# Sample attention in steps of 512 keys with a maximum each, and three edits beside it, in a decoder step

## The chip, the cores and the metric

The kernel runs on one core of a Trainium2 chip. Its engines each work through their own instructions in order: TensorE (PE; its weight loads are listed apart, as PEld), VectorE (DVE), ScalarE (ACT), GpSimd (POOL) and SyncE (SP, which here only issues transfers). They wait for each other by semaphores. The metric is the device time of one execution in microseconds (us), lower is better; a time is quoted as the median of several runs.

## The reference

One step of a decoder layer, for 1024 prompt tokens of one sequence and for 8 sample sequences of 8 new tokens each, which have 2048 past tokens in paged caches:

```python
x = ffn_half(x, ...ffn1)                                   # x + 0.5 * (silu(h @ wg) * (h @ wu)) @ wd
q, kc, vc, ks, vs, kw, vw, gates, z, xbc, dtr = split_proj(rmsnorm(x) @ w_in)
o_att = g0 * o_cmp + g1 * o_sel + g2 * o_win               # 8 query heads, 2 KV heads, width 64
y_ssm = rmsnorm_per_group(ssd(...) * silu(z)) * ssm_norm   # Mamba-2 scan, 8 heads
x = x + concat(o_att, y_ssm) @ w_out
x = ffn_half(x, ...ffn2)                                   # and a final RMSNorm
```

Attention has three branches, each a softmax of its own. The compressed branch looks at summaries of blocks of 32 keys (127 of them for a sample sequence). Its probabilities rank the blocks of 64 keys, and the selected branch attends to the best 16 of them (`select_blocks`, `top_k`). The window branch attends to the last 512 keys. Sigmoid gates weigh the three. A softmax is `exp(s - max(s)) / sum`, so for several pieces of the keys, each with its own maximum, the numerators and sums have to be brought to one maximum before they are added. In the Mamba part `y * silu(z)` is normalised by the mean of its squares over each of two groups of 256 channels.

## The kernel before, in words

Feature rows lie on the 128 partitions, tokens on the free axis. The stages in time are: FFN1; from 753 us the projections by w_in, with the Mamba scan from 899 us and the gating from 1050 us among them; from 1176 us prompt attention with the compression of the sample caches in it (to 1583 us); sample attention with w_out in it (1583 to 1815 us); FFN2 and the last norm. Who runs when on an engine is set by a scheduler that reads the program with a modelled timeline, within what the pools' buffer counts allow; on the chip each engine then keeps that order. Matmuls of float32 are made of three (`mm3`, L237 to L239): each operand is split into a high part, made by a cast (`whi`, ACT), and a low part, the difference (`wlo`, a subtraction by `split`, L257). `sub`, `copy` and `scale` (L257, L254, L266) take the engine as a letter from the table `KN`: 'v' DVE, 'a' ACT, 'p' POOL.

**Sample attention** takes the 8 sequences as 4 pairs; a pair's 2 x 8 tokens x 8 heads are the 128 rows. For a pair:

- `choose` (L1821 to L1873) computes gates and compressed scores, and ranks the blocks by comparing all pairs of 31 block scores on 128x961 tiles: `cm` (greater, L1862), `ce` (equal, L1863), then `ce * tri` and `cm + ce` on POOL (L257), a row sum `rk` (L1867) and a mask `msk`, which PE transposes (`a_ps`, L1872). All four run ahead of the scores.
- `rows_in` (L1881) fetches keys and values in pieces of 512 keys for a sequence, into `schk`, 10 buffers: the window by a plain transfer on SP, the four pieces of the 2048 past keys by gathers that POOL issues (L1887). The gathers don't depend on `choose`; unselected blocks are masked in the scores.
- `scores` (L1894) works by branch. For each piece PE transposes the keys (`kT_ps`, copied to `skT` by ACT), multiplies (`s_ps`, two PSUM banks) and adds the mask (L1919); DVE adds the position bias and takes the maximum (L1922). After all four pieces (and the 8 new tokens per sequence, L1929) one maximum, one exp over 2112 columns on ACT (L1934), a sum, its reciprocal, the gate, and one scaling of S on DVE (L266).
- `values` (L1951) transposes S piece by piece (`sPT_ps`, one bank, shared with `a_ps`), copies (`sPT`) and adds the products into `so`; `compressed` (L1940) adds that branch and `outputs` (L1977) writes `qT`.

**w_out** (`out_w`, L2026; `out`) runs as PE's filling in the same stage: w_out comes in 32 pieces (the last 8 behind sample attention), loaded through SP into `raw`, a tile of two buffers which the squares of x (`x2_sq`, L2063) and rows of x on their way from and to DRAM (`xD`, L2092, L2095) use too. Low halves go to POOL and DVE in turn.

**Scan.** `BD`, one tile of 96x2x4x128, holds the decay terms as blocks, in three bf16 parts for two halves of the chunks (L1052 to L1058). The first matmul of the scan, `ar` (L1098), reads it.

**Gating** (`gate`, L1189): z is loaded (`za`, one buffer), multiplied onto y, and y's squares go into `ysq`, a buffer of the tag `nat`, which also holds rows on the way to the output; four `yn` matmuls (L1203) per chunk then sum them over the partitions.

Of the kernel before, what the change touches and what calls it, by code (L numbers as in the profile page):

```python
# [17 lines left out]
P = 128  # L18
# [15 lines left out]
PAST = 2048  # L34
B0AT = (0, 2, 4, 6)
EARLY = {(0, 0): (0, 128), (1, 0): (640,), (0, 1): (), (1, 1): (768,)}
KN = {'Bt': 'a', 'cb': 'a', 'de': 'vv', 'ea': 'pp', 'st': 'p', 'hT': 'v', 'xm': 'p', 'yz': 'v', 'ysq': 'a', 'kT': 'aa', 'sPT': 'v', 'S': 'vv', 'ce': 'p', 'cm': 'p', 'pcT': 'v', 'msk': 'a', 'osb': 'av', 'q': 'sspss', 'pb': ['apppaapp', 'apppappp', 'apppappp', 'apvpappp', 'apppapvp', 'appvappp', 'vpvvvpvv', 'pvvvvvvv'], 'pc': 'p', 'ob': 'aa', 'QA': 'aapv', 'QB': 'pv', 'chp': 'ap', 'th': 'aa', 'qt': (2, 7, 6, 5, 4, 3, 1, 0), 'cs': [3, 0, 2, 1, 1, 0, 1, 0]}
# [42 lines left out]
def hybrid_step(ctx: ExitStack, tc: tile.TileContext, *aps):  # L80
# [868 lines left out]
    def mamba_setup(K, K2, Q, acs_bank):  # L949
# [98 lines left out]
        BD = K.tile([96, 2, 4, P], BF16, name="BD", bufs=1)  # L1048
        r = Q.tile([96, 2, P], F32, name="bd_r", bufs=1)
        for u in range(3):  # L1050
            b = Q.tile([96, 2, P], BF16, name="bd_b", bufs=1)
            nc.vector.tensor_copy(b, r if u else q[:96])  # L1052
            d = slice(32 * u, 32 * u + 32)
            for z in range(2):
                nc.vector.tensor_tensor(BD[d, z], b[d, z:z + 1].to_broadcast([32, 4, P]),
                                        hm[d, :, None].to_broadcast([32, 4, P]), op=OP.mult)
            if u < 2:
                nc.vector.tensor_tensor(r, r if u else q[:96], b, op=OP.subtract)  # L1058
# [3 lines left out]
    def scan(K, dt, dA, U, Us, Bof, bm, mU, mUs, nacs, dend, cdec, dsk, sel, BD):  # L1062
# [5 lines left out]
        for c in range(9):  # L1068
# [25 lines left out]
            for g in range(2):  # L1094
                ar = b1("ar")
                arv = ar.rearrange("p (h l) -> p h l", h=4)
                if c < 8:
                    nc.tensor.matmul(ar, sel[:, 2 * (c % 4) + g:2 * (c % 4) + g + 1].to_broadcast([96, P]),  # L1098
                                     BD[:, c // 4].rearrange("p h l -> p (h l)"), start=True, stop=True,
# [89 lines left out]
    def gate(K, yr, c):  # L1189
# [5 lines left out]
        sq = K.tile([P, 4, P], F32, name="ysq", tag="nat")  # L1195
        if KN["ysq"] == "a":
            nc.scalar.activation(sq[:, :, :L], yT[:, :, ts], AF.Square)
        else:
            sub(KN["ysq"], sq[:, :, :L], yT[:, :, ts], yT[:, :, ts], OP.mult)
# [508 lines left out]

    def sample_attention():
        def b1(name):  # L1710
            return PSS.tile([P, 512], F32, name=name, tag="sPT_ps" if name == "a_ps" else name,
                            bufs=2 if name in ("kT_ps", "s_ps") else 1)
# [94 lines left out]
        for s4 in range(4):  # L1807
# [6 lines left out]
                                base=3, channel_multiplier=4)  # L1814
        grow = SC.tile([P, 4, 3], F32, name="grow")
# [59 lines left out]
        vals, probs = {}, {}  # L1875
# [5 lines left out]
        def rows_in(pr, br):  # L1881
            for s4 in range(4 if br == 0 else 1):
                for b in pair(pr):
                    chk = KS.tile([P, 4, 256], F32, name="schk")
                    vals[b, br, s4] = chk
                    if br == 0:
                        nc.gpsimd.indirect_dma_start(  # L1887
                            out=chk.rearrange("p s c -> p (s c)"), out_offset=None, in_=ch_sel,
                            in_offset=bass.IndirectOffsetOnAxis(ap=idx4[:, b, s4:s4 + 1], axis=0))
                    else:  # L1890
                        QUEUES[KN["q"][4]].dma_start(chk.rearrange("p s c -> p (s c)"),
                                          A["cache_win"][0, b].rearrange("(c s) k g d -> c (s k g d)", s=4))
# [418 lines left out]
```

## Time and profile before

| | |
|---|---|
| median of 3 runs | 2588.24 us (2579.92 to 2588.73) |
| the profiled execution | 2587.16 us |
| its span on the core | 2585.4 us |
| granted TensorE clock, mean | 0.966 |
| busy: PE / DVE / ACT / POOL | 2450.2 / 1751.9 / 1112.2 / 464.0 us |
| sample attention with w_out | 1583 to 1815 us |

The span is the time from the first to the last instruction on the core; the execution's time has a little around it. Busy times are sums of the instructions' durations, and "idle before" is what an engine stood before an instruction, with the event that ended it. The granted clock is a share of TensorE's full clock: at 0.5 a matmul takes twice as long.

### The profile page before, as it was taken

What the parts mean: (1) busy time and instruction counts of PE and PEld (TensorE: products, weight loads), DVE (VectorE), ACT (ScalarE), POOL (GpSimd) and SP (SyncE); (2) the same over time, 40 slices, a digit from 0 to 9 for tenths busy, and PEclk for the clock granted to TensorE, in tenths of its full rate; (3) what the DMA queues carried; (4) which work ended last, traced back from release to release, by engine and by line L of the source; (5) the groups of instructions that cost most, each with busy time, mean ns of one, the idle gap of its engine ahead of it and who ended that gap; (6) DMA issues with size and microseconds to landing.
All of it is one profiled execution on the core that took longest, in us unless ns stands there. A gap on an engine that the chain in (4) does not pass through costs nothing.

```text
span 2585.4 us, 48000 instructions
## 1 busy us (share of the span) xinstructions
PE 2450.2 (95%) x19011; PEld 2254.0 (87%) x19011; DVE 1751.9 (68%) x3610; ACT 1112.2 (43%) x2433; POOL 464.0 (18%) x549
## 2 busy tenths in 40 slices
PE   6999999999999999999999998788799999999998
PEld 5999999999999899897777775465699999999998
DVE  6776767677786645655666667644776767768776
ACT  7544444432152253225666664222444444443113
POOL 0000000011143334333443343322000000001110
PEclk9999999999999999899999997798799999999999
DMA  4334444596642224321101003176233434459754
GB/s 162 122 138 159 136 145 145 187 371 241 229 170 80 90 80 115 109 85 64 66 34 66 33 34 131 41 236 213 82 110 115 166 123 159 150 170 375 269 204 148
DMA packets 226269, 371.91 MB, mean 144 GB/s; under 512 B 18173, under 2 KB 143785, under 8 KB 224892
## 3 DMA queue, kind: packets, MB, share of 16 engines
q1 hardware_dynamic: 207112, 311.92, 35.5%
q0 software_dynamic: 7600, 38.59, 4.2%
q10 hardware_dynamic: 11332, 18.33, 1.9%
q8 instruction: 150, 2.46, 0.4%
q14 instruction: 75, 0.61, 0.1%
HBM read 250.84 MB, written 122.07 MB: 144 GB/s over the span
## 4 chain that ended last, share of the span: by engine, by line
PE 82%; DVE 8%; DMA 5%; ACT 3%; issue 1%; POOL 1%; SPq 0%; ACTq 0%; DVEq 0%; POOLq 0%
PE gY L352 6%; PE gY L353 6%; PE gY L351 6%; PE dq L609 6%; PE dq L608 6%; PE dq L610 6%; PE gX L352 5%; PE gX L351 5%; PE gX L353 5%; PE o L1688 3%; PE pT L1679 3%; DMA raw<-in_w_out_dram 1%; PE s L1641 1%; PE cA L1566 1%; PE xbc L237 1%
## 5 line engine op out<-in xcount | busy, mean ns | idle before, releaser
L609 PE MATMUL dq<-db,da 128*128 128x256 f32 (+1 forms) x1232 | 352.7, 287 | 0.3 <-DVE da L257 0.3
L610 PE MATMUL dq<-db,da 128*128 128x256 f32 (+1 forms) x1232 | 352.4, 287 | 0.0
L608 PE MATMUL dq<-db,da 128*128 128x256 f32 (+1 forms) x1232 | 349.1, 288 | 3.4 <-DMA db<-GD 1.7
L257 POOL TENSOR_TENSOR ds<-dw 128x512 f32<-128x512 f32 x22 | 29.0, 1319 | 1208.9 <-DMA dw<-in_ffn_wd_dram 512.8
L617 DVE TENSOR_TENSOR xT<-xT,dq 128x256 f32<-128x256 f32 (+1 forms) x456 | 186.8, 432 | 84.1 <-PE dq L610 82.4
L608 PEld LDWEIGHTS dq<-db,da 128*128 128x128 f32 x1232 | 229.8, 188 | 4.5 <-DVE Cc L371 1.4
L610 PEld LDWEIGHTS dq<-db,da 128*128 128x128 f32 x1232 | 232.2, 189 | 0.0
L609 PEld LDWEIGHTS dq<-db,da 128*128 128x128 f32 x1232 | 231.2, 188 | 0.6 <-DVE da L257 0.5
L254 ACT CAST whi<-ws 128x512 fp32r<-128x512 f32 x156 | 96.4, 622 | 209.2 <-PE gY L353 144.1
L257 DVE TENSOR_TENSOR wlo<-raw,whi 128x512 fp32r<-128x512 f32 x168 | 115.8, 694 | 85.1 <-ACT whi L254 84.8
L254 ACT CAST da<-ds 128x512 fp32r<-128x512 f32 x88 | 52.6, 624 | 236.6 <-PE dq L610 93.5
L254 ACT CAST whi<-raw 128x512 fp32r<-128x512 f32 x184 | 113.7, 624 | 75.2 <-DMA raw<-in_w_out_dram 37.6
L1657 ACT ACTIVATE pb<-s,mx 128x256 f32<-128x256 f32 (+3 forms) x192 | 105.2, 553 | 73.1 <-DVE mx L1655 38.2
L257 DVE TENSOR_TENSOR wlo<-ws,whi 128x512 fp32r<-128x512 f32 x156 | 106.7, 687 | 42.8 <-ACT whi L254 42.3
L1679 PEld LDWEIGHTS pT<-ident,pb 128*128 128x128 f32 x528 | 59.8, 143 | 43.4 <-issue 39.5
L1654 DVE TENSOR_REDUCE mx<-s 128x1 f32<-128x384 f32 (+2 forms) x128 | 66.7, 536 | 43.2 <-PE s L1646 32.2
L351 PE MATMUL gX<-B6h,whi 128*128 128x256 f32 (+1 forms) x320 | 92.2, 289 | 1.3 <-ACT Cc L358 1.3
L264 POOL TENSOR_TENSOR pb<-pb,sm 128x640 f32<-128x640 f32 (+7 forms) x70 | 84.9, 1236 | 45.8 <-DVE sm L1664 43.6
L352 PE MATMUL gX<-B6h,wlo 128*128 128x256 f32 (+1 forms) x320 | 92.5, 289 | 0.5 <-DVE wlo L257 0.5
L351 PE MATMUL gY<-B3h,whi 128*128 128x256 f32 (+1 forms) x320 | 91.5, 287 | 1.4 <-ACT whi L254 1.4
L352 PE MATMUL gX<-B7h,wlo 128*128 128x256 f32 (+1 forms) x320 | 91.8, 287 | 0.3 <-DVE wlo L257 0.3
L353 PE MATMUL gX<-B6l,whi 128*128 128x256 f32 (+1 forms) x320 | 92.0, 288 | 0.0
(705 smaller groups left out, 8648.8 us busy)
## 6 DMA issues: line engine op xcount, KB each, us to landing
db<-GD SPq DMA_DIRECT2D x42, 1632.0 KB
GD<-Cc SPq DMA_DIRECT2D x154, 272.0 KB
GD<-his SPq DMA_DIRECT2D x84, 272.0 KB
raw<-in_ffn_wg_dram SPq DMA_DIRECT2D x22, 1024.0 KB
raw<-in_ffn_wu_dram SPq DMA_DIRECT2D x22, 1024.0 KB
dw<-in_ffn_wd_dram SPq DMA_DIRECT2D x44, 512.0 KB
GD<-hp SPq DMA_DIRECT2D x70, 272.0 KB
db<-GD SPq DMA_DIRECT2D x14, 1088.0 KB
```

The source lines that it names most:

```text
L254: return nc.scalar.copy(out, src) if eng == "a" else ENGINES[eng].tensor_copy(out, src)
L257: ENGINES[eng].tensor_tensor(out, x, y, op=op)
L264: nc.gpsimd.tensor_tensor(out, x, by.to_broadcast(list(x.shape)), op=OP.mult)
L351: nc.tensor.matmul(q, ah[:, k], b_, start=first, stop=False, skip_group_check=True)
L352: nc.tensor.matmul(q, al[:, k], b_, start=False, stop=False, skip_group_check=True)
L353: nc.tensor.matmul(q, ah[:, k], c_, start=False, stop=(k == 3), skip_group_check=True)
L608: nc.tensor.matmul(q, x, bh[:, u, o], start=first, stop=False, skip_group_check=True)
L609: nc.tensor.matmul(q, y, bh[:, u, o], start=False, stop=False, skip_group_check=True)
L610: nc.tensor.matmul(q, x, bl[:, u, o], start=False, stop=(u == np_ - 1), skip_group_check=True)
L617: nc.vector.tensor_tensor(x, x, q, op=OP.subtract if i == 4 else OP.add)
L1657: nc.scalar.activation(pb[:, st:st + pn], s, AF.Exp, bias=mx[:, 0:1], accum_out=part[:, hh_, i:i + 1])
L1679: nc.tensor.transpose(tq_[:kn, P * hh_:P * hh_ + P], src, ident)
```

## The change

**Steps.** Sample attention becomes 20 steps: for each pair the window (k = 0) and then the four pieces of 512 past keys (k = 1 to 4); the new tokens go with k = 0 and k = 4, which are 576 wide. Each step has its own maximum (`nm[:, k]`), exp and sum (`rs[:, k]`), and S isn't scaled. Its values go to 64 columns of their own in the bank `so`, which one bf16 matmul with a zero operand clears for a pair; 320 to 383 hold the compressed branch. At a pair's end `outputs` takes the least of the negated maxima of k = 1 to 4, makes factors by an exp, sums, divides, applies the gates and adds the five pieces with `scalar_tensor_tensor`. Values of a step are written behind the scores of the next. Rows are fetched five steps ahead. `choose` for a pair stands behind k = 1 of the pair before it.

**Banks.** `s_ps` has one bank instead of two, and `a_ps` one of its own; `kT_ps` keeps two, `sPT_ps` and `so` one each.

**GpSimd.** `ce` and `cm` go to DVE. So do w_out's low halves, except for the last 8 pieces, where POOL takes every second one. **w_out's buffers**: `raw` has three buffers for w_out alone, and `xs` two for the squares and x's rows.

**Gating.** Squares are written over `za` by ACT, DVE adds them in pairs, and there are two `yn` matmuls instead of four. **Scan.** `BD` becomes two tiles, made one after the other.

```diff
-KN = {... 'ysq': 'a', 'S': 'vv', 'ce': 'p', 'cm': 'p', ...}
+AHEAD = 5
+KN = {... 'ce': 'v', 'cm': 'v', ...}
...
+        BD = []
+        def blocks_of(z):
+            D = K.tile([96, 4, P], BF16, name=f"BD{z}", bufs=1)
+            r = Q.tile([96, P], F32, name="bd_r", bufs=1)
+            for u in range(3):
+                b = Q.tile([96, P], BF16, name="bd_b", bufs=1)
+                src = r if u else q[:96, z]
+                nc.vector.tensor_copy(b, src)
+                if u < 2:
+                    nc.vector.tensor_tensor(r, src, b, op=OP.subtract)
+                d = slice(32 * u, 32 * u + 32)
+                nc.vector.tensor_tensor(D[d], b[d, None, :].to_broadcast([32, 4, P]),
                                         hm[d, :, None].to_broadcast([32, 4, P]), op=OP.mult)
+            BD.append(D)
...
-        sq = K.tile([P, 4, P], F32, name="ysq", tag="nat")
-            nc.scalar.activation(sq[:, :, :L], yT[:, :, ts], AF.Square)
+        nc.scalar.activation(za[:, :, :L], yT[:, :, ts], AF.Square)
+        nc.vector.tensor_tensor(za[:, ::2, :L], za[:, ::2, :L], za[:, 1::2, :L], op=OP.add)
         q = side("yn")
         for g in range(2):
-            for i in range(2):
-                nc.tensor.matmul(q[:L, g:g + 1], sq[:, 2 * g + i, :L], ones[:, :1], start=(i == 0), stop=(i == 1),
-                                 skip_group_check=True)
+            nc.tensor.matmul(q[:L, g:g + 1], za[:, 2 * g, :L], ones[:, :1], start=True, stop=True,
+                             skip_group_check=True)
...
+        def scores(pr, k, nm, rs):
+            n = 512 + (TS if k in (0, 4) else 0)
+            S = K.tile([P, 576], F32, name="S", bufs=4)
+            mx = K.tile([P, 2], F32, name="smxs", bufs=4)
...
+            nc.vector.tensor_reduce(nm[:, k:k + 1], mx[:, :2 if n > 512 else 1], axis=AX.X, op=OP.max, negate=True)
+            nc.scalar.activation(S[:, :n], S[:, :n], AF.Exp, bias=nm[:, k:k + 1], accum_out=rs[:, k:k + 1])
+            return S, n
...
+        def outputs(pr, O, nm, rs):
+            nc.vector.tensor_reduce(t[:, 0:1], nm[:, 1:5], axis=AX.X, op=OP.min)
+            nc.scalar.activation(cf[:, 1:5], nm[:, 1:5], AF.Exp, scale=-1.0, bias=t[:, 0:1])
...
             osb = K.tile([P, 64], F32, name="osb")
-            copy("a", osb, O[:, :64])
+            copy("a", osb, O[:, 320:384])
+            for k in range(5):
+                nc.vector.scalar_tensor_tensor(osb, O[:, 64 * k:64 * k + 64], cf[:, k:k + 1], osb, op0=OP.mult,
+                                               op1=OP.add)
...
+        for i, (pr, k) in enumerate(steps):
+            if i + AHEAD < len(steps):
+                rows_in(*steps[i + AHEAD])
+            now = scores(pr, k, *state[pr][:2])
+            if held is not None:
+                finish()
+            held = pr, k, *now
+            if k == 1 and pr < 3:
+                choose(pr + 1)
+        finish()
...
-        raw = WA.tile([P, 576], F32, name="raw", bufs=2)[:, :512].rearrange("p (k f) -> p k f", k=4)
+        raw = WA.tile([P, 4, P], F32, name="raw", bufs=3)
...
-        split(hi, lo, raw, "pv"[m % 2 == 0])
+        split(hi, lo, raw, eng)
...
-    ws = [out_w(WA, 0, m) for m in range(KD)]
+    ws = [out_w(WA, 0, m, "vp"[m % 2]) for m in range(KD)]
```

How the order moves, at three places. POOL in sample attention: before, gathers, low halves and the choices' two passes stand in one queue (the first eight gathers are those of the first pair).

```order
L1887 DMA schk<-in_cache_sel_dram,idx_18705 128x1024 x8
L257 TENSOR_TENSOR wlo<-raw,whi 128x512
L257 TENSOR_TENSOR ce<-ce,tri 128x961
L257 TENSOR_TENSOR cm<-cm,ce 128x961
L257 TENSOR_TENSOR wlo<-raw,whi 128x512 x2
L257 TENSOR_TENSOR ce<-ce,tri 128x961
L257 TENSOR_TENSOR cm<-cm,ce 128x961
L257 TENSOR_TENSOR wlo<-raw,whi 128x512 x3
```

After, the same stretch of POOL's queue is all its 32 gathers, and then the four low halves of the last pieces:

```order
L1895 DMA schk<-in_cache_sel_dram,idx_18702 128x1024 x32
L258 TENSOR_TENSOR wlo<-raw,whi 128x512 x4
```

The passes on `ce` and `cm` now stand on DVE, between a step's drain of scores (L1927, written ISA), copies of transposed S (L255), additions onto x (L2071) and a low half; this is the second pair's choice:

```order
L1870 TENSOR_TENSOR cm<-imp 128x961
L1871 TENSOR_TENSOR ce<-imp 128x961
L1856 MEMSET pg 128x1
L258 TENSOR_TENSOR ce<-ce,tri 128x961
L1927 ISA S,smxs<-s_ps,bsel 128x512
L1927 ISA smxs 128x1
L2071 TENSOR_TENSOR xT_20106<-xT_20106,wout 128x512
L258 TENSOR_TENSOR cm<-cm,ce 128x961
L258 TENSOR_TENSOR wlo<-raw,whi 128x512
L255 COPY sPT<-sPT_ps 128x512
```

PE at the stage's end, from the last w_out matmul of the stage to the norm's first (`nps`), after the change: values of four pieces (`so`, 16 matmuls each) follow each other, and scores of the last two steps stand before them.

```order
L240 MATMUL wout<-ol,whi 128x288
L1973 MATMUL so<-schk,sPT 32x64 x16
L1959 MATMUL sPT_ps<-ident,S 64x128
L1918 MATMUL s_ps<-skT,QS 64x512 x2
L1924 LDWEIGHTS mskT
L1924 MATMUL s_ps<-oneh,mskT 128x512
L1970 MATMUL so<-vtok,sPT 32x64 x4
L1963 MATMUL sPT_ps<-ident,S 128x128 x4
L1932 MATMUL s_ps<-ksTs,QS 64x64 x2
L1973 MATMUL so<-schk,sPT 32x64 x16
L1963 MATMUL sPT_ps<-ident,S 128x128 x4
```

Before, the transposes of keys, three more score matmuls and five pieces' values stood there (they are in the rows of time that the next section shows).

More of the change, by code (lines that the diff above doesn't have):

```diff
@@ L1706, in hybrid_step @@
     PSS = Es.enter_context(pool("sa_ps", bufs=1, space=PSUM))
+    PSA = Ahead(PSS)
+    for nm_ in ("a_ps", "s_ps", "sPT_ps", "so", "kT_ps"):
+        PSA.first(nm_, [P, 512], 2 if nm_ == "kT_ps" else 1)
     def sample_attention():
         def b1(name):
-            return PSS.tile([P, 512], F32, name=name, tag="sPT_ps" if name == "a_ps" else name,
-                            bufs=2 if name in ("kT_ps", "s_ps") else 1)
+            return PSA.tile(name, [P, 512], 2 if name == "kT_ps" else 1)
         ch_sel = A["cache_sel"][0].rearrange("n (c s) k g d -> (n c) (s k g d)", s=4)
@@ L1873, in choose @@
             copy(KN["msk"], mskT[:, pr], q[:32, :P])
-        vals, probs = {}, {}
+        vals = {}
         def group_rows(pr):
             return [(slice(64 * (b % 2) + 32 * g, 64 * (b % 2) + 32 * g + 32), b, g) for b in pair(pr) for g in range(2)]
-        def rows_in(pr, br):
-            for s4 in range(4 if br == 0 else 1):
-                for b in pair(pr):
[L1884 to L1892, printed above, removed]
@@ new lines, in rows_in @@
+        def rows_in(pr, k):
+            for b in pair(pr):
+                chk = KS.tile([P, 4, 256], F32, name="schk")
+                vals[b, k] = chk
+                if k:
+                    nc.gpsimd.indirect_dma_start(
+                        out=chk.rearrange("p s c -> p (s c)"), out_offset=None, in_=ch_sel,
+                        in_offset=bass.IndirectOffsetOnAxis(ap=idx4[:, b, k - 1:k], axis=0))
+                else:
+                    QUEUES[KN["q"][4]].dma_start(chk.rearrange("p s c -> p (s c)"),
+                                      A["cache_win"][0, b].rearrange("(c s) k g d -> c (s k g d)", s=4))
@@ L1948, in compressed, with values @@
                                  skip_group_check=True)
             return O
-        def values(pr, br, O, last):
-            nt = 4 if br == 0 else 1
-            S = probs.pop(br)
-            for s4 in range(nt + 1):
-                new = s4 == nt
+        def values(pr, k, S, n, O):
+            for new in range(2 if n > 512 else 1):
                 q = b1("sPT_ps")
@@ L2061, in x2_sq @@
         else:
-            sq = WA.tile([P, 576], F32, name="raw", bufs=2)[:, :c]
+            sq = WA.tile([P, 576], F32, name="xs", bufs=2)[:, :c]
             nc.scalar.activation(two(sq), x, AF.Square)
             nc.vector.tensor_tensor(acc2[z], acc2[z], sq, op=OP.add)
-    for _ in sample_attention():
-        pass
+    sample_attention()
     PO = Es.enter_context(pool("psum_wo", bufs=2, space=PSUM))
@@ L2089, in hybrid_step @@
         w = out_w(WA, 1, m)
[L2090 removed]
+        xs = WA.tile([P, 576], F32, name="xs", bufs=2)
         for b in range(2):
```

154 lines of the change are left out of this document (66 added, 88 removed).

## The prediction

> **What bounds the kernel now.** I read first the page (span, share of TensorE, chain), then the table by stretches, then the waits, and last the order of time at the places that these name.
>
> ```profile
> span 2585.4 us, 48000 instructions
> PE 2450.2 (95%) x19011; PEld 2254.0 (87%) x19011; DVE 1751.9 (68%) x3610; ACT 1112.2 (43%) x2433; POOL 464.0 (18%) x549
> PEclk9999999999999999899999997798799999999999
> ```
>
> TensorE (PE) is busy for 95% of the span and its clock is near full but in a few slices: 7 at slices 25 and 26, 8 and 7 at slices 28 and 29. A slice is 64.6 us, so these five begin at 1551 us and hold sample attention, where I looked by stretches. The columns are start and end, length, then busy us of PE, PEld, DVE, ACT and POOL, the granted clock, the DMA share and GB/s.
>
> ```profile
> 1583.00:1601.00 18.00, 12.65 (x56) 6.32 (x55) 9.31 (x29) 8.31 (x21) 8.90 (x9) 0.81 0.97 348
> 1601.00:1643.00 42.00, 39.07 (x182) 26.44 (x183) 33.55 (x75) 15.72 (x31) 15.79 (x8) 1.00 0.32 95
> 1643.00:1684.00 41.00, 24.35 (x75) 16.86 (x74) 21.13 (x40) 5.99 (x13) 11.45 (x6) 0.64 0.07 20
> 1684.00:1787.00 103.00, 90.16 (x1012) 65.17 (x1012) 44.54 (x114) 32.35 (x56) 30.00 (x29) 0.96 0.73 234
> 1787.00:1815.00 28.00, 18.47 (x249) 10.71 (x248) 11.23 (x31) 5.99 (x11) 1.27 (x1) 0.70 0.54 174
> ```
>
> Two stretches are poor: 1643 to 1684, where PE is busy for 24.35 of 41 us at a clock of 0.64 while DMA is all but idle (0.07), and 1787 to 1815, 18.47 of 28 at 0.70. In 1684 to 1787 PE still stands for 12.8 us. What ended the idle time, by waits (total us, times, longest):
>
> ```profile
> POOL wlo L257 <- ACT whi L254: 62.8, 9, 12.2
> POOL schk L1887 <- PE so L1974: 45.9, 6, 13.7
> PE wout L237 <- ACT whi L254: 12.1, 7, 4.0
> ACT raw L2063 <- DVE msk L1870: 21.0, 2, 10.5
> PE a_ps L1872 <- DVE msk L1870: 9.6, 3, 4.9
> PE sPT_ps L1963 <- DVE S L266: 4.4, 1, 4.4
> ```
>
> GpSimd (POOL) does gathers and the low halves of w_out in one queue: a low half waits for its high half (62.8 us), a gather for a buffer (45.9), and each holds up what is queued behind it. PE itself waits for the block choice's mask (9.6), for w_out's high half (12.1) and once for the scaling of S (4.4).
>
> **The first poor stretch.** The last three block choices run there one after another. One of them, from the chain of work, and PE beside it:
>
> ```profile
> 1648.51 1.16 DVE cm L1862
> 1650.88 2.25 POOL ce L257
> 1655.45 1.15 DVE rk L1867
> 1657.34 0.40 PE L1872 MATMUL a_ps<-ident,msk 128*32 128x128 f32 x1 [4.94 <-DVE msk L1870]
> 1661.60 0.63 PE L239 MATMUL wout<-ol,whi 128*128 128x512 f32 x1
> 1662.03 0.63 PE L237 MATMUL wout<-oh,whi 128*128 128x512 f32 x1
> 1642.74 0.39 PE L237 MATMUL wout<-oh,whi 128*128 128x512 f32 x1
> 1642.97 0.39 PE L238 MATMUL wout<-oh,wlo 128*128 128x512 f32 x1
> ```
>
> PE stands 4.94 us for the mask, and its matmuls then come 0.43 us apart instead of 0.23. Counted at full clock the stretch has 24.35 x 0.64 = 15.6 us of PE work, in 41 us.
>
> After the change, the choice for a pair stands among the steps of the pair before it, so this work can lie between transposes and scores. The pace I take for the whole of 1643 to 1787 (144 us) comes from the rows beside it: 15.6 + 90.16 x 0.96 = 102.2 us of work at full clock. The stretch from 1684 on needs 103 us for 86.6, 1.19 per us of work; 1601 to 1643 needs 42 for 39.07, 1.075. At 1.075 the 144 us become 110 (-34), at 1.19 they become 122 (-22). What raises the pace is VectorE (DVE):
>
> ```profile
> L257 POOL TENSOR_TENSOR wlo<-raw,whi 128x512 fp32r<-128x512 f32 x13 | 18.3, 1405 | 63.0 <-ACT whi L254 62.8
> L257 DVE TENSOR_TENSOR wlo<-raw,whi 128x512 fp32r<-128x512 f32 x14 | 10.7, 764 | 8.7 <-ACT whi L254 8.7
> L266 DVE TENSOR_SCALAR S<-S,mxs 128x2112 f32<-128x2112 f32 x4 | 6.9, 1720 | 0.1
> L266 DVE TENSOR_SCALAR S<-S,mxs 128x576 f32<-128x576 f32 x4 | 2.1, 526 | 0.1
> L1934 ACT ACTIVATE S<-S,mxs 128x2112 f32<-128x2112 f32 x4 | 8.2, 2058 | 6.2 <-DVE mxs L1933 6.2
> L1929 DVE CUSTOM_DVE_ANT_0 S<-s_ps,bnew 128x64 f32<-128x64 f32 x8 | 1.8, 219 | 0.0
> L1922 DVE CUSTOM_DVE_ANT_0 S<-s_ps,bsel 128x512 f32<-128x512 f32 x16 | 11.0, 688 | 8.9 <-PE s_ps L1919 8.7
> DMA to landing us min/median/max: 4.4/5.8/9.1
> ```
>
> Added to DVE: 12 low halves at 0.764 (9.2 us) and 8 operations on ce and cm; the trace has no such pass with two wide inputs on DVE, so between the 1.16 of L1862 (same output) and POOL's 2.25, and I take 1.16, the same engine (9.3). The recombination is 20 passes of 128x64 out of PSUM at 0.219 and some 28 tiny ones, which I bound by nothing and the same 0.219 and take at 0.16 (8.9). Removed: 4 x 1.72 + 4 x 0.526 (-9.0); small maxima and reciprocals go both ways and are costed at nothing. DVE goes from 119.8 us (its five stretches) to about 138, in some 200 us: it still has room, but in an in-order queue with more in it. Against that, PE's 12.1 us for high halves shrinks with a third w_out buffer. I take 1.205, nearer the measured 1.19: 123, and 1 us for the four matmuls that zero the sums (bounds 0 and 4 x 0.4, the mask transpose). **Term 1: -20** (bounds -34 and, at 1.33, -7). The new maxima and the extra exps, 20 instead of 8, go on DVE and ACT beside PE; the exp is cut from 2.06 us per 2112 keys to a fraction per 512, off PE's path while PE has other columns to do. Gathers now stand alone in POOL's queue and are issued five steps ahead, before a transfer is needed; at 0.07 to 0.73 DMA share there is room, so I cost this at nothing. Without that cover it would be one landing, 5.8 us, per pair. The first two stretches hold the loads (0.97) and a PE that is already full: 0.
>
> **The second poor stretch.** From the last w_out matmul to the norm's first matmul:
>
> ```profile
> 1786.76 0.29 PE L239 MATMUL wout<-ol,whi 128*128 128x288 f32 x1
> 1800.70 1.11 PE L1963 MATMUL sPT_ps<-ident,S 128*128 128x128 f32 x4 [4.37 <-DVE S L266]
> 1802.60 1.08 PE L1974 MATMUL so<-schk,sPT 128*32 128x64 f32 x32 [0.78 <-DVE sPT L254]
> 1803.62 1.12 PE L1963 MATMUL sPT_ps<-ident,S 128*128 128x128 f32 x4
> 1815.10 1.20 PE L807 MATMUL nps<-ones,acc 128*128 128x1 f32 x5 [0.76 <-DVE qT L1987]
> ```
>
> 28.3 us: one exp over four chunks and a scaling stand between the last scores and the first values, then five value chunks at 2.92 us each (1800.70 to 1803.62, at half clock). Now only the last two steps' scores and four value chunks follow the last w_out matmul: 4 x 2.92 = 11.7, two steps' scores at 1 each (estimates, from a chunk's share of the rows here), the value matmuls of the pair's first chunk and the new rows, 2 more, and the recombination, 5 x 0.22, a transpose and the 0.76 that the norm waits for qT, some 2.5: about 18 to 19. **Term 2: -9** (bounds -3, if the exp waits stay, and -12 at full clock).
>
> **Blocks for the scan and the gating.** The two tiles of the decay blocks:
>
> ```profile
> 894.28 1.28 DVE L1055 TENSOR_TENSOR BD<-bd_b,hm 32x512 bf16<-32x512 bf16 x2
> 899.16 1.01 PE L1098 MATMUL ar<-BD,sel 96*128 96x512 bf16 x2 [6.39 <-DVE BD L1055]
> ```
>
> PE waits 6.39 us for six block passes of 0.64 and what lies between. The first matmuls now need only three passes: 3 x 0.64 = 1.9 less, and half of the casts' work, 0.6. **Term 3: -2.5** (bounds 0 and -5, when PE's half clock behind it goes too). In the gating, squares need no free output buffer any more:
>
> ```profile
> 1055.93 1.15 ACT L1197 ACTIVATE ysq<-yT 128x512 f32<-128x512 f32 x2 [6.30 <-DMA out_dram<-nat]
> 1054.00:1058.00 4.00, 2.25 (x17) 2.02 (x16) 1.77 (x7) 1.72 (x4) 0.52 (x1) 0.92 0.16 41
> 1058.00:1068.00 10.00, 10.00 (x49) 10.00 (x48) 2.81 (x6) 2.43 (x4) 2.54 (x2) 0.50 0.45 121
> ```
>
> The squares waited 6.30 us for an output transfer, PE stood 1.75 of 4 us, and then ran ten us at 0.50, which costs 5 us of full-clock work. All of it back is -7; but z's one buffer is now held until the sums are made, and the next z load with what is queued behind it on SP comes later, up to +4. DVE's pair sum (0.7 to 1.3 us by the wide passes above) adds itself to that chain. **Term 4: -5** (bounds -10, with the next slow stretch, and +4). [...]
>
> Sum: -20 - 9 - 2.5 - 5 = **-36.5**. The profiled execution took 2587.16 us (1.8 around its span), 1.1 below the median of 2588.24. So 2587.2 - 36.5 = 2550.7, on the median's basis **2552 us**.
>
> **The rivals.** *DVE's queue becomes the pace.* A step's score drain (0.69) and the copy of its transposes stand in order behind the choice's five passes of 1.16 and w_out's low halves. For: the DVE sum grows by 18 us and ce and cm come in the middle of steps. Against: 138 us of about 200, and other PE work between. At a pace of 1.33 (term 1 is -7) with the other terms the sum is -23, 2565; with the gating's +4 2574. *PE never stands long enough to lose its clock.* For: the half clock follows each poor place shown. Then pace 1.075: -33, tail -11, scan and gating -11: 2533. *The choice and its GpSimd passes were not what held the stage* but w_out's loads, whose waits are the same whoever splits them: term 1 is -2, the tail -5, half of terms 3 and 4 -4, in all -11: 2577, no change that can be told. *The other side: one bank for scores.* Before, two banks let the next scores start while DVE drains; now there is one. It is used 20 + 8 times, and the bank for the transposes of S as often. If each holds PE for one drain and its hand-over, the 0.78 us of the row at 1802.60, that is 56 x 0.78 = 44 us, 2596; if the clock in the stage also falls to the 0.81 of the first stretch, 102.2 x (1/0.81 - 1/0.96) = 20 more, 2615. It decides from 36.5 / 56 = 0.65 us per use. Against it: no row shows PE waiting for that drain, the transposes' bank was single before, and values of the step before and w_out columns stand between two uses. [...]
>
> **How the numbers follow.** Forecast 0.47, DVE's queue 0.20, full clock 0.13, loads 0.12, one bank 0.08. The range goes from 2530 (the pace of 1.075 with the bounds of the small terms) to 2580 (loads). The likeliest case alone: 2541 to 2563. 0.5% is 13 us, about what a measurement of this kernel can tell from no change: faster means under 2575. The forecast, the first two rivals and a quarter of loads are faster, 0.83; the rest of loads, and little of the last, the same, 0.10; slower 0.07.
>
> **What would show it.** Right: the norm's first matmul comes near 1779 instead of 1815; no stretch in the stage under a clock of 0.8 but the tail; the waits of PE on the mask and of POOL's wlo gone; the tail's 28.3 near 19; PE's wait on the first blocks about 4 us; and no squares waiting on an output transfer. Wrong: PE waiting on a score drain or on a DVE copy for tens of us, gathers waiting to land, or a stretch of z loads before the yn matmul. If the stage keeps its 230 us with less POOL time, the third rival holds.

## The result

The changed kernel takes **2546.19 us** (median of 4 runs, 2545.51 to 2548.51), the kernel before 2586.31 us beside it (4 runs): a ratio of **0.985, 95% interval 0.983 to 0.987**, 40 us less. Forecast were 2552 us, with 2530 to 2580 as the range. The sum came out; its parts did not, as the table below shows. All medians and ratios are of runs in the chip's usual state, which leaves out one run of the experiments, 8164.42 us of the kernel "changed, old banks".

The page of the changed kernel, the lines that answer to those of before:

```profile
span 2546.8 us, 48004 instructions
PE 2439.3 (96%) x18979; PEld 2241.6 (88%) x18979; DVE 1759.6 (69%) x3676; ACT 1116.8 (44%) x2461; POOL 430.4 (17%) x530
PEclk9999999999999999999999999899899999999999
```

TensorE is busy 11 us less with nearly as many instructions. More of them ran at full clock: no slice is at 7 now, two are at 8. Sample attention by stretches (start and end, length, busy us of PE, PEld, DVE, ACT, POOL, granted clock, DMA share, GB/s):

```profile
1584.00:1604.00 20.00, 15.50 (x50) 8.03 (x50) 12.05 (x44) 6.41 (x22) 9.32 (x10) 0.50 0.51 179
1604.00:1644.00 40.00, 38.58 (x287) 24.89 (x285) 31.61 (x78) 17.96 (x39) 1.90 (x2) 0.90 0.66 214
1644.00:1684.00 40.00, 40.00 (x322) 27.08 (x311) 27.16 (x74) 19.23 (x40) 6.92 (x6) 1.00 0.52 159
1684.00:1724.00 40.00, 36.16 (x350) 26.74 (x349) 27.43 (x69) 15.30 (x31) 10.53 (x8) 0.91 0.72 232
1724.00:1765.00 41.00, 39.76 (x409) 30.43 (x398) 25.65 (x76) 14.32 (x32) 9.37 (x9) 1.00 0.75 239
1765.00:1780.00 15.00, 9.09 (x207) 5.52 (x206) 8.86 (x31) 2.86 (x8) 0.00 (x0) 0.97 0.57 180
```

The hole is gone: from 1604 to 1765 us PE stands for 6.5 of 161 us, at 0.9 to full clock. The poor row is now the first: the end of prompt attention runs at half clock, and sample attention begins later than before.

To see where time went, I cut every profile at four instructions: w_in's first matmul, prompt attention's first score matmul (`s`) and last value matmul (`o`), and the norm's first (`nps`). For the kernel before and then the changed one, the stretch of prompt attention and that of sample attention:

```profile
1176.40:1590.10 413.70, 397.31 (x2642) 286.37 (x2641) 273.87 (x683) 266.76 (x716) 163.36 (x246) 0.97 0.11 42
...
1590.10:1815.10 225.00, 179.16 (x1542) 123.30 (x1541) 116.08 (x275) 65.63 (x122) 61.83 (x48) 0.86 0.52 169
```

```profile
1174.00:1603.80 429.80, 408.66 (x2641) 291.18 (x2641) 275.05 (x683) 267.36 (x716) 164.56 (x249) 0.95 0.12 44
...
1603.80:1780.00 176.20, 163.79 (x1547) 114.65 (x1545) 120.72 (x327) 69.66 (x150) 28.71 (x25) 0.96 0.66 209
```

Sample attention lost 48.8 us: 33.4 in which PE stood, and 15.4 of busy time for the same number of matmuls (1542 and 1547), the clock being 0.96 instead of 0.86. Prompt attention, in which no line was changed, grew by **16.1 us**. With the other stretches (all from one profile each, in us):

| kernel | w_in to `s` | prompt | sample | after `nps` | span |
|---|---|---|---|---|---|
| before | 422.9 | 413.7 | 225.0 | 770.3 | 2585.4 |
| changed | 418.2 | 429.8 | 176.2 | 766.8 | 2546.8 |
| difference | -4.7 | +16.1 | -48.8 | -3.5 | -38.6 |

The rest of the difference, +2.3, is in front of w_in, where the two programs do the same.

### The profile page after: what moved, and what is told of

Same layout as the page of the kernel before. It is cut to its first block, busy times and chain, and to the rows that moved or that the text cites. A ratio compares the mean times of both kernels' runs of the same rounds, so it can differ in the third digit from the quotient of the medians.

```text
span 2546.8 us, 48004 instructions
## 1 busy us (share of the span) xinstructions
PE 2439.3 (96%) x18979; PEld 2241.6 (88%) x18979; DVE 1759.6 (69%) x3676; ACT 1116.8 (44%) x2461; POOL 430.4 (17%) x530
## 4 chain that ended last, share of the span: by engine, by line
PE 83%; DVE 8%; ACT 3%; DMA 3%; issue 1%; POOL 0%; ACTq 0%; DVEq 0%; SPq 0%; POOLq 0%
PE gY L353 6%; PE gY L354 6%; PE gY L352 6%; PE dq L609 5%; PE dq L610 5%; PE dq L611 5%; PE gX L353 4%; PE gX L354 4%; PE gX L352 4%; PE o L1691 3%; PE pT L1682 3%; PE s L1644 1%; PE cA L1569 1%; PE xbc L238 1%; PE cA L1571 1%
## 5 line engine op out<-in xcount | busy, mean ns | idle before, releaser
L255 ACT CAST whi<-ws 128x512 fp32r<-128x512 f32 x156 | 96.4, 622 | 210.5 <-PE gY L354 144.7
L258 DVE TENSOR_TENSOR wlo<-raw,whi 128x512 fp32r<-128x512 f32 x180 | 123.0, 688 | 79.2 <-ACT whi L255 78.9
L255 ACT CAST da<-ds 128x512 fp32r<-128x512 f32 x88 | 52.8, 626 | 236.9 <-PE dq L611 92.5
L255 ACT CAST whi<-raw 128x512 fp32r<-128x512 f32 x184 | 113.9, 625 | 65.9 <-PE gY L354 20.0
L1682 PE MATMUL pT<-ident,pb 128*128 128x128 f32 x528 | 90.8, 290 | 3.5 <-ACT pt L255 1.5
L353 PE MATMUL gY<-B3h,wlo 128*128 128x256 f32 (+1 forms) x320 | 91.7, 287 | 0.2 <-DVE wlo L258 0.2
L353 PE MATMUL gY<-B2h,wlo 128*128 128x256 f32 (+1 forms) x320 | 91.8, 287 | 0.0
```

The lines of the kernel that those rows point to most:

```text
L255: return nc.scalar.copy(out, src) if eng == "a" else ENGINES[eng].tensor_copy(out, src)
L258: ENGINES[eng].tensor_tensor(out, x, y, op=op)
L353: nc.tensor.matmul(q, al[:, k], b_, start=False, stop=False, skip_group_check=True)
L1682: nc.tensor.transpose(tq_[:kn, P * hh_:P * hh_ + P], src, ident)
```

## The experiments

Three questions were open: what makes prompt attention longer; what carries the gain in sample attention (the steps, the place of the choices, GpSimd's freed queue, the buffers or the banks); and what the parts give together. Each run's profile was cut as above; "sample + after" adds the last two stretches, because a kernel can move w_out columns behind `nps`.

| kernel | median, us | ratio to before [95%] | w_in to `s` | prompt | sample + after |
|---|---|---|---|---|---|
| before | 2586 to 2592 | 1 | 422.9 | 413.7 | 995.3 |
| changed, again | 2544.8 | 0.984 [0.981, 0.987] | 418.5 | 428.5 | 940.5 |
| changed, old gating | 2538.9 | 0.980 [0.979, 0.982] | 427.3 | 413.7 | 940.7 |
| before, new gating and blocks | 2603.5 | 1.005 [1.003, 1.007] | 416.8 | 430.5 | 997.5 |
| changed, work back on GpSimd | 2547.2 | 0.983 [0.981, 0.985] | 419.3 | 429.8 | 945.0 |
| changed, old buffers | 2557.1 | 0.987 [0.985, 0.989] | 419.5 | 428.0 | 950.5 |
| changed, choices ahead | 2540.3 | 0.984 [0.982, 0.987] | 414.9 | 430.1 | 935.6 |
| before with the steps alone | 2551.3 | 0.988 [0.985, 0.990] | 419.4 | 412.6 | 961.8 |
| changed, old banks | 2579.4 | 0.997 [0.995, 0.999] | 417.4 | 428.3 | 968.7 |
| before, new banks | 2566.2 | 0.991 [0.988, 0.994] | 417.9 | 415.4 | 975.2 |
| before, new banks, buffers, GpSimd | 2561.2 | 0.989 [0.986, 0.992] | 417.8 | 412.6 | 968.7 |
| changed, old gating, choices ahead | 2533.1 | 0.979 [0.976, 0.982] | 427.3 | 410.8 | 939.2 |
| changed, rows two steps ahead | 2542.4 | 0.982 [0.979, 0.985] | 416.7 | 430.7 | 942.0 |

The kernel before was timed beside each group of four; its median was 2588.3, 2586.7 and 2591.8 us.

### The gating and prompt attention

The changed kernel with the gating's lines as before:

```diff
-        nc.scalar.activation(za[:, :, :L], yT[:, :, ts], AF.Square)
-        nc.vector.tensor_tensor(za[:, ::2, :L], za[:, ::2, :L], za[:, 1::2, :L], op=OP.add)
+        sq = K.tile([P, 4, P], F32, name="ysq", tag="nat")
...
+            nc.scalar.activation(sq[:, :, :L], yT[:, :, ts], AF.Square)
...
```

> The changed kernel with the gating as before (squares into a buffer of the tag nat, four matmuls per chunk); PE's order in prompt attention is then that of the kernel before. Theory 1: the gating edit cost more than it gave, because with it the scheduler laid out prompt attention anew, and from its first score matmul to its last value matmul it took 16 us longer (429.8 against 413.7). Then this kernel is faster than the changed one by about 11 to 14 us: 2532 to 2536, with that stretch near 414. Rival: the longer stretch comes from sample attention's own setup and banks reaching into it, and the gating's gain of 2 to 5 us is lost here: 2548 to 2551, with the stretch near 430.

Measured: 2538.9 us, ratio 0.980, and prompt attention back at 413.7 us. Theory 1 holds for that stretch. The time fell by less than the 16 us, because the stretch from w_in to `s` grew to 427.3 us: with the old gating and the two block tiles together the scheduler lays out that stretch in a third way.

The kernel before with the gating's and the blocks' edits (both as in the diff of the change) and nothing else:

> The kernel before with the gating edit and the two block tiles, and nothing else; PE's order in prompt attention is then that of the changed kernel. Theory 1 (the gating edit's new layout of prompt attention costs about 16 us, the two edits' own gain is 4 to 5): 2586 + 11 = about 2597, slower than before. Rival (the prediction's terms 3 and 4, and no cost in prompt attention): 2579.

Measured: 2603.5 us (9 runs), ratio 1.005 [1.003, 1.007]: **slower than before** by half a percent, as theory 1 had it (2597), and clear of the rival. Its prompt attention:

```profile
1173.80:1604.30 430.50, 408.35 (x2641) 290.60 (x2641) 275.14 (x683) 268.00 (x716) 164.96 (x248) 0.95 0.12 45
```

The same 430 us and the same clock of 0.95 as in the changed kernel, without any of sample attention's edits. PE's order in prompt attention is word for word the same in all kernels with the new gating and blocks, and the same in all with the old gating as in the kernel before; between the two it differs throughout. So the gating edit reaches prompt attention through the order that the scheduler works out. PE's waits for the scores' exp, in the kernel before and then in the changed one:

```profile
PE s L1641 <- ACT pb L1657: 5.5, 10, 1.1
```

```profile
PE s L1644 <- ACT pb L1660: 9.4, 15, 1.8
```

Most of the added waiting is in the last 40.1 us of the stretch, which are poor in both kernels. Without them these waits are 3.7 us before and 4.0 now, the longest 0.7 and 0.8, and the stretch is 373.6 us with 363.58 busy at a clock of 1.00 before, and 389.7 us with 376.98 busy at 0.97 now. So 13.4 of the 16.1 us are longer matmuls and 2.7 are idle time.

```profile
1176.40:1550.00 373.60, 363.58 (x2485) 264.45 (x2485) 241.14 (x559) 248.98 (x657) 147.68 (x220) 1.00 0.11 40
```

```profile
1174.00:1563.70 389.70, 376.98 (x2488) 272.16 (x2488) 246.53 (x569) 251.67 (x666) 147.91 (x221) 0.97 0.11 39
```

The longer matmuls are mostly the clock's doing. In the changed kernel's profile it is at 0.5 in five places of this stretch, and the 23.1 us for which PE is busy there would be 11.5 at full clock by the granted share, an estimate (w_out's matmuls of 512 columns follow each other by 0.43 us at 0.50 in the kernel before, by 0.23 us at 1.00). In the 6 us ahead of each place PE had stood for 1.1 to 1.5 us in all, never longer than 1.0 us at once. One of the five, the 6 us ahead of it and then the place itself:

```profile
1370.21:1376.21 6.00, 4.64 (x30) 3.52 (x28) 3.54 (x10) 3.35 (x11) 0.50 (x3) 1.00 0.53 227
1376.21:1383.03 6.82, 6.15 (x25) 5.44 (x26) 4.44 (x11) 4.08 (x12) 3.90 (x5) 0.50 0.00 1
```

In the kernel before as much standing passed without a half clock, 1.56 of 6 us and then the next six:

```profile
1218.00:1224.00 6.00, 4.44 (x31) 3.17 (x31) 4.18 (x12) 3.77 (x11) 0.91 (x3) 1.00 0.00 0
1224.00:1230.00 6.00, 6.00 (x51) 5.54 (x49) 3.15 (x8) 3.67 (x11) 5.85 (x4) 1.00 0.01 3
```

The same stretch in the kernel before with the new gating and blocks, and then in the changed kernel with the old gating:

```profile
1173.80:1564.20 390.40, 376.53 (x2487) 271.40 (x2486) 246.60 (x568) 252.13 (x665) 148.44 (x221) 0.97 0.11 39
```

```profile
1182.30:1555.90 373.60, 363.56 (x2484) 264.48 (x2484) 241.04 (x560) 248.87 (x657) 147.81 (x220) 1.00 0.11 40
```

In the first PE is idle for 3.9 us more than in the kernel before and busy for 13.0 more, at 0.97; in the second both are as before, at 1.00.

### GpSimd's queue

The choices' two passes and w_out's low halves go back to POOL:

```diff
-KN = {... 'ce': 'v', 'cm': 'v', ...}
+KN = {... 'ce': 'p', 'cm': 'p', ...}
...
-        split(hi, lo, raw, eng)
+        split(hi, lo, raw, "pv"[m % 2 == 0])
...
```

> The changed kernel with the choices' two passes and w_out's low halves in POOL's queue again, as before. Theory A (the gain in the stage comes from the order in steps, with each choice among the steps): POOL has 9 us of passes and 18 us of low halves back in a stage of 180 us, 2546 to 2556. Theory B (the gain comes from GpSimd's queue being free for gathers): most of the stage's 49 us is lost, 2570 to 2590.

Measured: 2547.2 us, ratio 0.983 against 0.985 and 0.984 of the changed kernel. That GpSimd only gathers is worth nothing that can be told here, with three buffers for w_out; theory B falls. The sample stretches together are 2 to 4.5 us longer, so a small gain is not excluded.

With the old two buffers it is another matter. The kernel with the steps alone, where GpSimd has its work and w_out two buffers, takes 961.8 us from sample attention to the end; the changed kernel with the old buffers, where VectorE does that work, takes 950.5 (one profile each). In the first, PE waits for GpSimd's low halves (in the second 1.7 us, once):

```profile
PE wout L239 <- POOL wlo L258: 5.9, 4, 3.7
```

So the long wait of POOL for the high halves before, 62.8 us, can't be called free: a low half that comes late holds a buffer, and w_out's next loads waited for it (the kernel before, SP's queue):

```profile
SPq L2028 <- POOL wlo L257: 32.9, 7, 10.6
```

### w_out's buffers

```diff
-        raw = WA.tile([P, 4, P], F32, name="raw", bufs=3)
+        raw = WA.tile([P, 576], F32, name="raw", bufs=2)[:, :512].rearrange("p (k f) -> p k f", k=4)
...
-            sq = WA.tile([P, 576], F32, name="xs", bufs=2)[:, :c]
+            sq = WA.tile([P, 576], F32, name="raw", bufs=2)[:, :c]
...
```

> The changed kernel with one tile of two buffers for w_out, squares and rows of x, as before. Theory A (order in steps): w_out's loads come later by a few us, 2548 to 2555. Theory C (the buffers are what feeds PE): PE's waits for high halves, 12.1 us in the kernel before, come back and the clock falls with them, 2558 to 2575.

Measured: 2557.1 us, at the border between the two. By stretches it costs 8 to 10 us, and the mechanism is theory C's: from sample attention to the end of w_out PE waits again for high halves.

```profile
PE wout L238 <- ACT whi L255: 15.2, 8, 5.5
```

Sample attention itself is no longer (172.8 us); what its w_out columns didn't get done there follows behind `nps` (777.7 instead of 766.8 us).

### The place of the choices

All four choices are written ahead of the first step, as before:

```diff
-        choose(0)
+        for pr in range(4):
+            choose(pr)
...
-            if k == 1 and pr < 3:
-                choose(pr + 1)
```

> The changed kernel with all four choices ahead of the first step, as before. Theory A1 (the gain in the stage is that PE no longer stands for the choices): a stretch like that of 1643 to 1684 comes back, 41 us for 15.6 us of work at full clock, so about +20: 2566. Theory A2 (the gain is the steps' own order, scores of a step beside values of the step before, with a short exp and no scaling): the choices' chain on DVE hides behind w_out's columns, +0 to +6: 2546 to 2552.

The changed kernel beside it:

> The changed kernel itself, as the measure for the three beside it on the same chip: 0.985 of the kernel before, 2544 to 2550.

Measured: 2540.3 us against 2544.8, ratios 0.984 and 0.984. Theory A1 falls: nothing comes back. In its one profile PE is even fuller, and the norm's first matmul comes 169.0 us after the last `o`, not 174.5 to 176.2:

```profile
1600.60:1760.00 159.40, 156.34 (x1430) 110.04 (x1428) 114.89 (x305) 67.58 (x145) 24.49 (x25) 0.98 0.67 215
```

### The steps without the other edits

The kernel before with sample attention in steps and its banks, and gating, blocks, GpSimd's work and buffers as before:

> The kernel before with sample attention in steps and its banks alone: gating, block tiles, GpSimd's work and w_out's buffers as before. Theory A: the steps carry the gain, and the other edits add up as measured one by one against the changed kernel (gating undone -9, buffers undone +10, GpSimd undone 0, blocks undone +2.5): about 2550. Rival: the edits need each other (gathers behind low halves and passes on POOL wait for loads that come late with two buffers): 2565 or more.

Measured: 2551.3 us, where the single effects add up to 2550, and the rival by its time is out. But the sum came out in part by luck. From sample attention to the end this kernel is 19 to 21 us longer than the changed one, where old buffers alone (8 to 10) and GpSimd's work alone (2 to 4.5) would make 10 to 14: these two do need each other. And taking back gating and blocks together gave 16 to 17 us in prompt attention and cost 1 ahead of it, where the sum had 6.5.

### The banks

The changed kernel with the banks of before:

```diff
-    for nm_ in ("a_ps", "s_ps", "sPT_ps", "so", "kT_ps"):
-        PSA.first(nm_, [P, 512], 2 if nm_ == "kT_ps" else 1)
+    for nm_ in ("s_ps", "sPT_ps", "so", "kT_ps"):
+        PSA.first(nm_, [P, 512], 2 if nm_ in ("kT_ps", "s_ps") else 1)
...
-            return PSA.tile(name, [P, 512], 2 if name == "kT_ps" else 1)
+            tag = "sPT_ps" if name == "a_ps" else name
+            return PSA.tile(tag, [P, 512], 2 if name in ("kT_ps", "s_ps") else 1)
```

> The changed kernel with the banks of before: two for scores, and the choices' bank shared with the transposes of S. The prediction's fourth rival priced one bank at up to 0.78 us in each of 28 uses. If a tenth of that shows, this kernel is 2 us faster, if a third, 7 us (2539). If the bank costs nothing, 2546, and if the sharing of the choices' bank with the transposes holds up values while a choice runs, slower by 2 to 6 us.

Measured: **2579.4 us**, ratio 0.997: outside everything that was expected. Whatever a second bank for scores may give, sharing the choices' bank with the transposes of S takes back 26 to 28 us of the stage's gain on top of it (in the profile, which is of a run of 2574.2 us). In its order of time one sees how: while a choice holds the bank, from its gates to its mask, no transpose of S can be issued, so no values either (here the bank's tile is called `sPT_ps` for both).

```profile
1752.41 0.40 PE L1834 MATMUL sPT_ps<-gates,E 64*128 64x24 f32 x2
1753.09 0.44 PE L1843 MATMUL sPT_ps<-kcTs,QS 128*64 128x127 f32 x4 [0.27 <-DVE nm L1937]
...
1758.04 0.63 PE L1855 MATMUL sPT_ps<-spc,G 128*128 128x127 f32 x2
...
1766.11 0.39 PE L1881 MATMUL sPT_ps<-ident,msk 128*32 128x128 f32 x1 [3.87 <-DVE msk L1879]
1766.85 1.11 PE L1964 MATMUL sPT_ps<-ident,S 128*128 128x128 f32 x4 [0.35 <-ACT mskT L255]
```

14.4 us pass from the gates to the next transpose of S, and the matmuls behind them run at half clock (1.11 us for four transposes against 0.66). This is the kernel before's first poor stretch too, only that there all four choices had the bank first:

```profile
1678.09 0.40 PE L1872 MATMUL a_ps<-ident,msk 128*32 128x128 f32 x1 [4.08 <-DVE msk L1870]
1678.87 0.58 PE L1943 MATMUL sPT_ps<-ident,pcg 128*127 128x128 f32 x1 [0.38 <-ACT mskT L254]
```

The first transpose for the values comes right behind the last choice's mask. The value matmuls of selected and window rows, first and last start, before and in the changed kernel:

```profile
L1974 PE MATMUL so<-schk,sPT x640: 219/219/317, 1685.9 to 1812.1; 128*32 128x64 f32 x160
```

```profile
L1973 PE MATMUL so<-schk,sPT x640: 219/219/244, 1622.5 to 1775.8; 128*32 128x64 f32 x160
```

So the test of the banks alone, in the kernel before:

```diff
-            return PSS.tile([P, 512], F32, name=name, tag="sPT_ps" if name == "a_ps" else name,
-                            bufs=2 if name in ("kT_ps", "s_ps") else 1)
+            return PSS.tile([P, 512], F32, name=name,
+                            bufs=2 if name == "kT_ps" else 1)
```

> The kernel before with one edit: the choices' tiles have a PSUM bank of their own and scores have one bank instead of two. Theory D (the sharing is what made the first poor stretch: in the order of the program all four choices take the shared bank ahead of the first values, so no values can run until the last choice is done): most of the stage's gain comes with it, 2586 - 25 to 35 = 2550 to 2562. Theory A (it is the steps): 2580 to 2592. The prediction's fourth rival (one bank for scores holds PE): slower, 2595 or more.

Measured: 2566.2 us, ratio 0.991 [0.988, 0.994]. The value matmuls:

```profile
L1974 PE MATMUL so<-schk,sPT x640: 219/219/317, 1611.2 to 1785.2; 128*32 128x64 f32 x160
```

The first ones now start at 1611.2 us instead of 1685.9, with the choices still ahead in the program, and the stage with what follows is 20 us shorter. This one edit gives some 23 of the 40 us. It is less than theory D's 25 to 35, much more than theory A's none, and not what the prediction's fourth rival had, 2595 or more.

With buffers and GpSimd's work in addition, still without steps:

> The kernel before with the banks, w_out's buffers and GpSimd's work as in the change, but sample attention by branch, with one maximum, one exp over 2112 keys and the scaling, and gating and blocks as before. Theory D: the steps themselves add little, so this comes within 6 us of the changed kernel with the old gating (2536 to 2539): 2536 to 2545. Theory A: the steps are worth 15 us or more beside the banks, 2551 or more.

Measured: 2561.2 us, and 968.7 us for the stage with what follows, where the kernels with steps have 935 to 945. Theory D falls here: beside banks, buffers and GpSimd's work the steps are worth some 26 to 28 us. The profile still shows what they took away, a wait for the scaling of S, and late stretches of the stage where PE stands and its clock is down:

```profile
PE sPT_ps L1963 <- DVE S L266: 4.5, 1, 4.5
```

```profile
1740.00:1760.00 20.00, 16.64 (x202) 10.64 (x201) 6.36 (x19) 3.91 (x8) 7.57 (x8) 0.67 0.59 186
1760.00:1780.00 20.00, 11.21 (x150) 6.43 (x152) 6.34 (x19) 3.90 (x5) 0.00 (x0) 0.76 0.45 144
```

By the table the 52 to 55 us of the stage with what follows are then: banks 20; steps 13 beside them (961.8 against 975.2); buffers and GpSimd's work 19 to 21 once there are steps (961.8 against 940.5 to 943.0), and only 6.5 without (968.7 against 975.2), which is not far above the 5 us by which profiles differ in one stretch (last section). Why the buffers and GpSimd's work give more beside the steps was not taken apart.

### How far ahead rows are fetched

```diff
-AHEAD = 5
+AHEAD = 2
```

> The changed kernel with rows fetched two steps ahead instead of five. The prediction costed the gathers at nothing because they are issued long before they are needed; a landing took 5.8 us (up to 9.1), and a step is now about 8 us (176 us for 20). Two steps ahead are still more than a landing: 2543 to 2548. Rival (a gather also waits for its buffer and for its turn in the transfers, so two steps are too few): PE's waits for gathered rows, 4.7 us now, grow to 15 or more and the time to 2555 or more.

Measured: 2542.4 us, ratio 0.982 [0.979, 0.985]: no loss. PE's waits for gathered rows:

```profile
PE kT_ps L1911 <- DMA schk<-in_cache_sel_dram,idx: 3.9, 3, 1.8
```

against 4.7 us with five steps. The rival falls, and the distance of five is not needed.

### The best of them

The changed kernel with the old gating and the choices ahead of the steps:

> The changed kernel with the gating as before and all four choices ahead of the steps. The two edits act in different stages, so they should add: 0.980 of the kernel before by the gating alone, and 0 to -5 us by the choices (the profile with the choices ahead had the stage 7 us shorter, its median was 4 us lower): 2529 to 2537. If the choices' place was noise, 2535 to 2539.

Measured: **2533.1 us**, ratio 0.979 [0.976, 0.982], against 0.980 [0.979, 0.982] with the old gating alone and 0.984 to 0.985 for the changed kernel. It beats both kernels; that the choices' place has a part in it is within the spread (939.2 against 940.7 us). It keeps the two block tiles, with which the stretch from w_in to `s` is 427.3 us; the kernels with old gating and old blocks have 417.8 to 422.9 there. Taking both edits back while keeping the new sample attention should therefore give some 4 to 9 us more. That kernel was not run.

## Why the prediction was right, and where it was not

**The total was right because two errors cancelled.** It said -36.5 us against the profiled execution; measured are -38.6 between the two profiles and -40 between the medians. Of that the stage of sample attention gave 48.8 us with 3.5 behind it, where terms 1 and 2 had 29, and prompt attention took 16.1 back, where the prediction had no term at all. That they met so closely is luck, and so is the norm's first matmul at 1780.0 us, where 1779 was forecast: the stage began 13.7 us later than before.

**Term 1 (the first poor stretch, -20) was too small, and for the wrong reason.** Its pace was 1.205 us per us of PE work at full clock. From 1604 to 1765 us the changed kernel has 147 us of such work (busy times by the clock of the four rows) in 161: 1.09, close to the 1.075 of the second rival, *PE never stands long enough to lose its clock*. In this stage that rival is what happened (the clock is 0.90 to 1.00 in these rows): its -33 - 11 = -44 stands beside the measured -48.8. The reason that the prediction gave was the choices in a row and their GpSimd passes. With the choices in a row (2540.3 us) and with the passes on GpSimd (2547.2 us) nothing came back. The row that it read, PE's 4.94 us wait for the mask, was the last link; what had emptied PE was that no values could be issued until the four choices had given the shared bank back. The description of the change lists the new bank for the choices, and the prediction put no price on it.

**Term 2 (the tail, -9) was too small in size.** From the last w_out matmul to the norm's first:

```profile
1765.11 0.40 PE L240 MATMUL wout<-ol,whi 128*128 128x288 f32 x1
...
1769.27 0.65 PE L1973 MATMUL so<-schk,sPT 128*32 128x64 f32 x32 [0.49 <-DVE sPT L255]
...
1771.30 0.65 PE L1973 MATMUL so<-schk,sPT 128*32 128x64 f32 x32 [0.78 <-DVE sPT L255]
...
1779.96 1.84 PE L808 MATMUL nps<-ones,acc 128*128 128x1 f32 x8 [0.76 <-DVE qT L1999]
```

14.9 us instead of 28.3, so -13.4. The order is as foreseen, four value chunks behind the last scores; the size that was wrong is the chunk, 2.03 us at full clock instead of 2.92 at half clock. Before, PE had stood for 4.37 us for the scaling of S ahead of these chunks; now its longest wait in the tail is 1.9 us, and the clock there is 0.97.

**DVE's work** was sized well and did not matter, so the first rival falls. The passes on `ce` and `cm` took 1.16 us each, as taken; a low half 0.686 us instead of 0.764; a recombination pass 0.281 instead of 0.219:

```profile
L258 DVE TENSOR_TENSOR wlo<-raw,whi 128x512 fp32r<-128x512 f32 x26 | 17.8, 686 | 1.4 <-ACT whi L255 1.3
L1990 DVE SCALAR_TENSOR_TENSOR osb<-so,cf,osb 128x64 f32<-128x64 f32 x20 | 5.6, 281 | 1.0 <-ACT osb L255 0.7
L258 DVE TENSOR_TENSOR ce<-ce,tri 128x961 f32<-128x961 f32 x4 | 4.6, 1160 | 0.0
```

DVE is busy for 120.7 of the stage's 176.2 us, and no wait of PE on it there is longer than 1.9 us.

**Term 3 (blocks, -2.5)**: PE's wait for the first blocks fell from 6.39 to 4.7 us, -1.7. By itself that is right, and somewhat over-sized. But the two tiles also change the order of what follows. Some 3 us behind the first blocks, where matmuls of w_in for z filled PE before, it now stands for the scan's state, and the gain is gone:

```profile
PE xs_ps L1083 <- DVE st L1148: 1.7, 1, 1.7
```

That wait is there with the old gating too, and with the two together the stretch from w_in to `s` is 4 to 9 us longer than in the kernels with both as before.

**Term 4 (gating, -5) failed.** The early stall went, and a later one of the same kind came. z's one buffer is now held until PE has made the sums, so the next z comes late, and the squares with it. But this wait of ACT did not make PE stand:

```profile
1058.91 0.63 ACT L1202 ACTIVATE za<-yT 128x512 f32<-128x512 f32 x1 [6.81 <-DVE yT L258]
```

PE's own wait, 5.3 us for the pair sum, came with the next z, and there the queues held the work: z was multiplied by 1069.2 us, but the square stood behind four casts on ACT, and the pair sum behind the subtractions that belong to these casts on DVE (until 1073.5):

```profile
1067.86 4.31 ACT L1341 CAST KA<-kvT 64x512 fp32r<-64x512 f32 x4 [0.61 <-PE pcB L239]
1072.19 0.63 ACT L1202 ACTIVATE za<-yT 128x512 f32<-128x512 f32 x1
...
1074.12 0.98 PE L1206 MATMUL yn<-ones,za 128*128 128x1 f32 x4 [5.35 <-DVE za L1203]
```

The stretches that the prediction had quoted:

```profile
1058.00:1068.00 10.00, 10.00 (x88) 10.00 (x87) 4.25 (x12) 3.25 (x6) 2.50 (x3) 1.00 0.20 55
1068.00:1080.00 12.00, 6.65 (x36) 6.45 (x36) 9.55 (x18) 6.95 (x10) 3.29 (x3) 0.72 0.47 130
```

The ten us at half clock are at full clock now, and ten us later PE stands for 5.3 us at 0.72; before, its waits at these `yn` matmuls were 1.7 and 2.0 us. The prediction had named the hold of z's buffer, with up to +4, and the pair sum in the chain, but not the queue of ACT, and took the gain for the likelier. From w_in to `s` the eight kernels with new gating and blocks have 414.9 to 419.5 us (mean 417.7) and the four with both as before 417.8 to 422.9 (mean 419.5): terms 3 and 4 together are -1.8, not -7.5. And the edit's price is in prompt attention. In the changed kernel's profile PE never stands there, without the last 40.1 us, for longer than 1.0 us at once, and the clock is at half in five places.

**The third rival (w_out's loads hold the stage)** had half of it right: the choices in a row and the passes on GpSimd were not by themselves what held the stage. But the loads were not either: the buffers' run gives 8 to 10 us, and 19 to 21 with GpSimd's work. **The fourth rival (one bank for scores holds PE)** did not come: in the changed kernel PE's idle time before all of the stage's score matmuls is 0.3 us, and that is for a mask; before the transposes of S it has none.

```profile
PE s_ps L1924 <- ACT mskT L255: 0.3, 1, 0.3
```

One bank for scores and one for the choices made the kernel before faster by 20 us in the stage, and the banks of before made the changed kernel slower by 26 to 28. What a second bank for scores would give by itself was not tried. The gathers, costed at nothing, cost nothing, with two steps ahead as with five.

## What to carry to other kernels

Where two uses share a buffer or a PSUM bank, read the time from the first request of the one to the first use of the other: a wait at the end of a chain can be the smallest part of what the sharing holds up, and one edit that gave the chain a bank of its own made the kernel before some 23 us faster, where the whole change gave 40. Where a scheduler sets the order, an edit is measured in every stretch behind it and not only in its own; cut each profile at the same few instructions, and take the edits back one by one. A part that looks right by its own waits, like the gating here, can cost more elsewhere than it gives.

## What the runs showed of the hardware that was not expected

PE's clock cost more in prompt attention than its idle time did: 2.7 us more of standing still, never longer than 1.0 us at once, went with 13.4 us more of busy time for the same matmuls in the changed kernel's profile, and 3.9 us more with 13.0 in that of the kernel before with the new gating and blocks. In the changed kernel's profile PE had stood for 1.1 to 1.5 us in all in the 6 us ahead of each half clock; in the kernel before it stood for 1.56 of 6 us and went on at 1.00. What decides it was not shown. And the same instructions in the same order are not the same time to the microsecond: from w_in to prompt attention, PE's order is the same in the kernel before and in the three kernels that keep its gating and blocks, and their profiles have 422.9, 419.4, 417.9 and 417.8 us there. Differences of 5 us in a stretch of one profile are no finding.
